# Prompt q and k split by tokens and transposed by DMA in a hybrid streaming step

## The chip, the cores and the metric

The kernel runs on one core of a Trainium2 chip. The metric is the device time of one execution in microseconds (us). Before the change it is 1780.86 us, the median of three runs (1780.17 to 1781.07).

The engines are named as the profile names them: PE is TensorE's matmul, PEld its loading of the stationary operand, DVE is VectorE, ACT is ScalarE, POOL is GpSimd, and SP is SyncE, which only issues transfers here.

## What is computed

One layer of a streaming encoder serves two groups of requests: a prompt of 1024 tokens and 8 samples of 16 tokens, 1152 tokens together. Cut to what the change touches:

```python
h = rms_norm(x, norm_g) * (1 + scale) + shift
proj = h @ w_in                       # q | k | v | gates | SSD inputs ...
q = rms_norm(q.reshape(b, s, 16, 64), q_norm_g)
k = rms_norm(k.reshape(b, s, 16, 64), k_norm_g)
# prompt: each chunk of 64 frames sees its own and the 8 chunks before it
s = einsum('bqhd,bkhd->bhqk', q, k) * 64 ** -0.5 + bias
p = softmax(where(mask, s, -1e30))
o_att = einsum('bhqk,bkhd->bqhd', p, v)
```

The rest of the layer is a gated attention projection, a Mamba-2 scan branch (SSD) with a causal convolution, merge gates, an output projection and the residual. Among the outputs are the last 512 normalised rows of k for the prompt and those of the 128 sample tokens. All of it is float32.

## The kernel before

**Products.** To keep float32 accuracy, a dense product is three fp16 matmuls: high by high, high by low and low by high parts, where the low part is the number less its rounded high part. `dense` (L683, matmuls in L698, L699 and L701) gives channels on the partitions in groups of 384 tokens, `dense_tok` (L737, L751 to L753) tokens on the partitions in blocks of 128. Weights come in 512 KB pieces, `w_split` and `halves` (L610, L619) make the parts, and `level` (L604) squares and sums each piece for a range test at the end.

**Attention by units.** `attention(u)` (L1171) handles two heads, eight units in all. It has four coroutines:

- `dense_gen` projects q, k and v for nine blocks of 128 tokens (eight of the prompt, one of the samples) into `qk` and `v`, then the next unit's gate `z`. The ninth block reuses the first block's place in `qk`, so its eviction is held until `st["turned"]` says that the first half has been turned.
- `prelude` (L1217 on) runs three times, for blocks 0 to 3, 4 to 7 and 8. Pool takes the inverse root of the mean square (`rsqrt_small`, L574) and multiplies the block by it (L1229). For the first two, TensorE transposes q and k (L1249, four 128x128 float32 transposes to a PSUM tile `g`), ScalarE writes the high part with the norm weight as its scale (L1250), once more the k output for the second half (L1252), and VectorE the low part (L1253). The high and low parts of q and k lie in four places `q` of 1024 columns, which are one set: the next unit gets them when this unit's last scores (m = 7) are done. The third run transposes the sample block (L1265) for sample attention and sends the k output (L1276).
- `prompt` (L1302) works in six rounds (`ROUNDS`): scores (L1404) into PSUM, VectorE's negated sum with the bias and its minimum (L1300), ScalarE's exponentials (L1297); then `turn` (L1321) splits the probabilities in two fp16 parts (L1332, L1333) and transposes them by DMA from SP (L1339), and `weigh` multiplies them with v (L1357).
- `sample` does the same for the samples in float32; its probabilities go through one DMA transpose as two 16-bit planes (L1481) and a copy that puts the planes together (L1483), before L1492.

After the eight units come the SSD head, the sixteen SSD pairs and the output stages, which the change does not touch.

**Order of the work.** The coroutines run against a made-up clock: `yield` adds a cost in ns, `pause` waits on that clock, and `walloc` waits for a place of a fixed layout (`L_ATT`, `L_Q`, `L_V` and others, tags such as `T` for v and z, `S` for scores, `Q` for `qk`). That gives a program order. The class `Order` (L137 to L408) then plans the order of each engine's instructions again with a cost model of engines, PSUM slots (three `d`, three `g`, one `s`) and DMA, looking at most 1200 units of work ahead; `cuts` mark where a score or weighing group begins. Each engine then runs its order strictly, waiting on semaphores.

A second kernel, `general_kernel`, follows behind a branch and is entered only if the range test fails; it is not entered here.

Of the kernel before, what the change touches and what calls it, by code (L numbers as in the profile page):

```python
# [16 lines left out]
P = 128  # L17
D = 1024
KT = D // P
NP = 1024  # L20
# [118 lines left out]
class Order:  # L139
# [89 lines left out]
    def build(self):  # L229
# [60 lines left out]
        opener = {}  # L290
        for name, (tag, us) in tiles.items():
# [120 lines left out]
def trunk_kernel(ctx: ExitStack, tc: tile.TileContext, h, again):  # L412
# [71 lines left out]
    L_Q = arena.set_layout(Q0, [("q", 4, 512)])  # L484
# [16 lines left out]
    L_ATT["Q"] = L_ATT["Q"] + arena.set_layout(E0 + 1184 + NP, [("Q", 1, 2048)])["Q"]  # L501
    L_ST = rarena.set_layout(0, [("b", 4, P), ("s", 2, P), ("x", 2, 2 * P)])

    def alloc(lay, tag, cols):
        if lay is L_H or lay is L_W or lay is L_W3 or lay is L_Q or lay is L_V:
            return Buf(arena, arena.alloc(lay, tag, cols // 2), cols, True)
# [538 lines left out]

    pinning[0] = False
# [124 lines left out]
    def attention(u):  # L1171
# [43 lines left out]
        def prelude():  # L1215
            bias = []
            for i, (t0, n) in enumerate(((0, 4), (4, 4), (8, 1))):  # L1217
# [10 lines left out]
                x = qk.ap[:, o0:o0 + 2 * n * P].rearrange("p (h d) -> p h d", d=HD)  # L1228
                nc.gpsimd.tensor_tensor(x, x, v[1].unsqueeze(2).to_broadcast([P, w, HD]), ALU.mult)  # L1229
                yield from pause(2600 + 190 * w + 640 * n)  # L1230
                if i == 0:

                    ops = []
                    for _ in range(4):
                        ops.append((yield from walloc(L_Q, "q", NP)))
                    qh, ql, kh, kl = st["ops"] = ops
                    ko = yield from walloc(lay, "S", 640)
# [4 lines left out]
                if i < 2:  # L1242
                    tok = slice(t0 * P, (t0 + n) * P)
                    for j, (hi, lo) in enumerate(((qh, ql), (kh, kl))):
                        g = par["qk_g"][:, j:j + 1]
                        ps = pg()
                        for s in range(n):
                            o = o0 + (2 * s + j) * P
                            nc.tensor.transpose(ps[:, s * P:(s + 1) * P], qk.ap[:, o:o + P], ident)  # L1249
                        nc.scalar.activation(hi.r[:, tok], ps, AF.Copy, scale=g)  # L1250
                        if i and j:
                            nc.scalar.activation(ko.ap[:, :512], ps, AF.Copy, scale=g)  # L1252
                        nc.vector.scalar_tensor_tensor(lo.r[:, tok], ps, g, hi.ap[:, tok], ALU.mult, ALU.subtract)  # L1253
                        yield 109 * n
                        yield from pause(600)
                    st["turned"] = True
                else:
# [10 lines left out]
                    for e in range(2):  # L1268
                        hs = slice(HD * e, HD * e + HD)
                        nc.scalar.activation(q4[hs, :, e, :], ps[hs, :P].rearrange("p (b s) -> p b s", s=NS), AF.Copy,  # L1270
                                             scale=par["qk_g"][hs, 0:1])
                    nc.scalar.activation(ko.ap[:, 512:], ps[:, P:], AF.Copy, scale=par["qk_g"][:, 1:2])
                    nc.scalar.activation(ks.ap, ps[:, P:], AF.Copy, scale=par["qk_g"][:, 1:2])
# [5 lines left out]
                    nb.free()  # L1279
                    st["bias"] = bias  # L1280
# [21 lines left out]
        def prompt():  # L1302
            yield from ready(lambda: "left" in st and prompts[0] == u)
            yield from until(st["t"])
            qh, ql, kh, kl = st["ops"]
# [41 lines left out]
            def weigh(js, po):  # L1347
# [2605 lines left out]
```

## Time and profile before

| | |
|---|---|
| median of three runs | 1780.86 us |
| the profiled execution | 1782.14 us, its span 1780.1 us |
| busy in the span: PE, DVE, ACT, POOL | 1743.0, 1234.7, 957.6, 351.1 us |
| DMA queue q1 (from SP), share of 16 engines | 51.7% |
| TensorE transposes of q and k (L1249) | 128 instructions, from 79.3 to 571.0 us |
| DMA transposes of probabilities (L1339, L1481) | 128 and 16 instructions, from 112.5 to 634.8 us |

The profile is of one execution. The span runs from the first to the last instruction. A group's row gives its line, engine, operation and shapes, then the busy time of the group and the mean of one instruction, then the engine's idle time just before the group and what ended it. Matmuls overlap, so the time that a matmul takes from the engine is read from the distance of two starts, not from its own length. The digits of the slices are tenths of a fortieth of the span (44.5 us).

### The profile page before, as it was taken

Reading aid. Unit: us, or ns where it says so; the run is one execution under the profiler, and the core shown is the slowest. Engines: PE = TensorE matmul, PEld = TensorE weight load, DVE = VectorE, ACT = ScalarE, POOL = GpSimd, SP = SyncE. Lnnn points to the kernel's source line nnn. Section 1 sums busy time; section 2 is a strip of 40 time slices with the busy share of each in tenths; the row PEclk is TensorE's granted clock in tenths of the full one; section 3 lists DMA queues with packets and bytes.
Section 4 is the critical chain, followed back from the end, with each engine's and each line's share of the span. In section 5 each row is a group of like instructions: output and inputs, shape, how many; then the busy total and the mean of one; then the engine's idle time right before and its main releaser. Section 6 shows DMA issues by size and latency. Waiting matters only on the chain.

```text
span 1780.1 us, 34953 instructions
## 1 busy us (share of the span) xinstructions
PE 1743.0 (98%) x13821; PEld 1095.7 (62%) x13821; DVE 1234.7 (69%) x2327; ACT 957.6 (54%) x1903; POOL 351.1 (20%) x624
## 2 busy tenths in 40 slices
PE   7999999999999999999999999999999999999997
PEld 4556555556655566666666666666666556666664
DVE  6468777885787957786768777777775526876722
ACT  8766556565565666545655666355552615332510
POOL 0233332224314101122212132222122100000000
PEclk9999999999999999999999999999999999999999
DMA  9248978887787984533444545434477734311321
GB/s 381 69 124 222 220 186 204 185 212 199 176 236 166 207 218 129 154 89 116 134 140 137 147 142 165 127 111 129 148 220 292 270 104 154 101 48 57 122 101 56
DMA packets 266565, 284.87 MB, mean 160 GB/s; under 512 B 199628, under 2 KB 200664, under 8 KB 266392
## 3 DMA queue, kind: packets, MB, share of 16 engines
q1 hardware_dynamic: 257432, 253.90, 51.7%
q0 software_dynamic: 8960, 28.65, 4.3%
q8 instruction: 110, 1.80, 0.4%
q14 instruction: 63, 0.52, 0.1%
HBM read 192.70 MB, written 43.66 MB: 133 GB/s over the span
## 4 chain that ended last, share of the span: by engine, by line
PE 81%; ACT 7%; DMA 5%; DVE 3%; POOL 2%; issue 1%; SPq 0%; DVEq 0%; ACTq 0%; POOLq 0%
PE d L698 17%; PE d L699 17%; PE d L701 17%; PE d L751 5%; PE d L753 4%; PE d L752 4%; PE g L1357 2%; PE s L1844 1%; PE g L1816 1%; ACT arena L1743 1%; DMA arena<-arena 1%; PE g L1864 1%; PE s L1404 1%; DMA arena<-in_wall_dram 1%; PE g L1404 1%
## 5 line engine op out<-in xcount | busy, mean ns | idle before, releaser
L698 PE MATMUL d<-arena 128*128 128x384 f16 x2172 | 709.9, 327 | 2.9 <-DVE arena L1714 2.7
L699 PE MATMUL d<-arena 128*128 128x384 f16 x2172 | 708.9, 326 | 0.0
L701 PE MATMUL d<-arena 128*128 128x384 f16 x2172 | 708.8, 326 | 0.0
L701 PEld LDWEIGHTS <-arena 128*128 128x128 f16 x2280 | 223.3, 98 | 148.0 <-issue 0.8
L698 PEld LDWEIGHTS <-arena 128*128 128x128 f16 x2280 | 223.7, 98 | 146.9 <-issue 8.6
L699 PEld LDWEIGHTS <-arena 128*128 128x128 f16 x2280 | 223.4, 98 | 140.6 <-issue 4.1
L608 ACT ACTIVATE arena<-arena 128x1024 bf16<-128x1024 f32 (+3 forms) x169 | 181.6, 1075 | 202.7 <-DMA arena<-in_wall_dram 138.9
L617 DVE SCALAR_TENSOR_TENSOR arena<-arena 128x1024 f16<-128x1024 f32 (+1 forms) x117 | 149.1, 1275 | 81.2 <-ACT arena L616 74.5
L616 ACT ACTIVATE arena<-arena 128x1024 f16<-128x1024 f32 (+1 forms) x117 | 122.4, 1047 | 126.3 <-PE d L699 111.1
L751 PE MATMUL d<-arena 128*128 128x384 f16 (+1 forms) x568 | 186.9, 329 | 0.7 <-ACT arena L1193 0.7
L753 PE MATMUL d<-arena 128*128 128x384 f16 (+1 forms) x568 | 186.1, 328 | 0.0
L752 PE MATMUL d<-arena 128*128 128x384 f16 (+1 forms) x568 | 186.1, 328 | 0.0
L1297 ACT ACTIVATE arena<-arena 128x640 f32<-128x640 f32 (+4 forms) x144 | 100.7, 701 | 66.1 <-DVE arena L1300 65.9
L1555 DVE SCALAR_TENSOR_TENSOR arena<-arena 128x1176 f32<-128x1176 f32 x72 | 107.2, 1488 | 1.9 <-ACT arena L1552 0.5
L1743 ACT ACTIVATE arena<-arena 128x128 f32<-128x128 f32 x288 | 89.7, 389 | 26.1 <-DMA arena<-acs_d 25.9
L1333 DVE SCALAR_TENSOR_TENSOR arena<-arena 128x640 f16<-128x640 f32 (+4 forms) x128 | 87.9, 720 | 0.0
L751 PEld LDWEIGHTS <-arena 128*128 128x128 f16 x576 | 56.2, 98 | 49.7 <-issue 16.4
L1225 POOL TENSOR_SCALAR arena<-arena 128x16 f32<-128x16 f32 (+1 forms) x24 | 11.2, 468 | 366.4 <-DVE arena L1198 331.4
L753 PEld LDWEIGHTS <-arena 128*128 128x128 f16 x576 | 56.4, 98 | 38.4 <-issue 0.2
L1192 ACT ACTIVATE arena<-d 128x256 f32<-128x256 f32 x71 | 26.9, 378 | 95.7 <-PE d L753 95.7
L752 PEld LDWEIGHTS <-arena 128*128 128x128 f16 x576 | 56.4, 98 | 32.7 <-issue 0.6
L1749 DVE TENSOR_TENSOR arena<-arena 128x1152 f32<-128x1152 f32 x32 | 45.9, 1434 | 39.2 <-ACT arena L1747 39.2
(242 smaller groups left out, 2619.5 us busy)
## 6 DMA issues: line engine op xcount, KB each, us to landing
arena<-in_wall_dram SPq DMA_DIRECT2D x85, 512.0 KB
arena<-acs_d SPq DMA_DIRECT2D x32, 576.0 KB
arena<-in_kc_dram SPq DMA_DIRECT2D x64, 256.0 KB
arena<-in_vc_dram SPq DMA_DIRECT2D x64, 256.0 KB
arena<-in_wada_dram SPq DMA_DIRECT2D x24, 512.0 KB
arena<-in_xT_dram SPq DMA_DIRECT2D x16, 576.0 KB
arena<-eacs_d SPq DMA_DIRECT2D x32, 288.0 KB
gate_d<-arena POOLq DMA_DIRECT2D x48, 192.0 KB, 4.2
```

What stands on the lines that cost most here:

```text
L608: keep(nc.scalar.activation(junk[:, :n], x, AF.Square, scale=scale * n ** -0.5, accum_out=sums[:, c:c + 1]))
L616: keep(nc.scalar.activation(hi, x, AF.Copy, scale=scale))
L617: keep(nc.vector.scalar_tensor_tensor(lo, x, scale, hi, ALU.mult, ALU.subtract))
L698: nc.tensor.matmul(ps, hi.r[:, wc], kh.r[:, tok], start=k == 0, stop=False)
L699: nc.tensor.matmul(ps, hi.r[:, wc], kl.r[:, tok], start=False, stop=False)
L701: nc.tensor.matmul(ps, lo.r[:, wc], kh.r[:, tok], start=False, stop=k == nk - 1)
L751: nc.tensor.matmul(ps, kh.r[:, tok], wh, start=k == 0, stop=False)
L752: nc.tensor.matmul(ps, kh.r[:, tok], wl, start=False, stop=False)
L753: nc.tensor.matmul(ps, kl.r[:, tok], wh, start=False, stop=k == KT - 1)
L1297: nc.scalar.activation(p, p, AF.Exp, bias=sm_[:, 4 + e:5 + e], scale=-1.0, accum_out=sm_[:, 6 + e:7 + e])
L1555: nc.vector.scalar_tensor_tensor(yc, r.ap[:, j:j + n], w4[:, i, j:j + 1], yc, ALU.mult, ALU.add)
L1743: nc.scalar.activation(me[e].ap[:, cs], me[e].ap[:, cs], AF.Relu, scale=-1.0, bias=a4[:, c, hds[e]:hds[e] + 1])
```

## The change

- q and k stay with tokens on the partitions until they are split. After the inverse root, Pool multiplies the block by the norm weights as well (a new tile `gains` with the weights repeated over the partitions, q's already times 64 ** -0.5). ScalarE makes the high part and VectorE the low part from `qk` into a new place `y` (two of them, 16 × 128 fp16 columns).
- Two DMA transposes per half (high and low parts, 128 × 1024 each) put them into one place `q` for all four operands, ordered by half of the tokens, part, q or k. TensorE's transposes of the prompt, their copies from PSUM and the k output's copy go. The sample block is still transposed by TensorE.
- The k output goes out with tokens on the partitions, from `qk`, in two stores per unit; the host puts the axes in order.
- The scores' pieces are cut at the border of the halves: 384 + 256, 256 + 384 and 128 + 512 columns for the query blocks 5, 6 and 7, where it was 320 + 320.
- Two more places `T` for v and z. The new places lie where the SSD part has places of its own later.
- `Order.build`: a `g` tile that begins with a marked group now counts the operands of all its matmuls before its first one may be placed.
- `general_kernel` transposes its k output once more, to the same layout; it isn't entered.

```diff
+            members[name] = tag, us
...
+        for name, (tag, us) in members.items():
+            if any(x.name in self.cuts for x in units[us[0]]["ins"]) and tag == "g":
+                for j in us[1:]:
+                    if units[j]["eng"] == "PE":
+                        for k, kind in units[j]["pred"].items():
+                            if k not in us and k < us[0]:
+                                units[us[0]]["pred"].setdefault(k, kind)
...
-    L_Q = arena.set_layout(Q0, [("q", 4, 512)])
+    L_Q = arena.set_layout(Q0, [("q", 1, 2048)])
...
+    L_Y = arena.set_layout(E0 + 1184 + NP + 2048, [("y", 2, 1024)])
+    L_ATT["T"] = L_ATT["T"] + arena.set_layout(E0 + 1184 + NP + 4096, [("T", 2, NT)])["T"]
+    L_G = arena.set_layout(E0 + 1184 + NP + 4096 + 2 * NT, [("g", 1, 256)])
...
+    gains = alloc(L_G, "g", 2 * P)
+    dma(gains.ap, h["gains"])
+    nc.vector.tensor_scalar(gains.ap[:, :P], gains.ap[:, :P], HD ** -0.5, None, ALU.mult)
...
-                x = qk.ap[:, o0:o0 + 2 * n * P].rearrange("p (h d) -> p h d", d=HD)
-                nc.gpsimd.tensor_tensor(x, x, v[1].unsqueeze(2).to_broadcast([P, w, HD]), ALU.mult)
-                yield from pause(2600 + 190 * w + 640 * n)
+                x = qk.ap[:, o0:o0 + 2 * n * P]
+                xh = x.rearrange("p (h d) -> p h d", d=HD)
+                nc.gpsimd.tensor_tensor(xh, xh, v[1].unsqueeze(2).to_broadcast([P, w, HD]), ALU.mult)
+                xt = x.rearrange("p (t c) -> p t c", c=2 * P)
+                nc.gpsimd.tensor_tensor(xt, xt, gains.ap.unsqueeze(1).to_broadcast([P, n, 2 * P]), ALU.mult)
+                yield from pause(2600 + 190 * w + 1100 * n)
...
                 if i < 2:
-                    tok = slice(t0 * P, (t0 + n) * P)
-                    for j, (hi, lo) in enumerate(((qh, ql), (kh, kl))):
-                        g = par["qk_g"][:, j:j + 1]
-                        ps = pg()
-                        for s in range(n):
-                            o = o0 + (2 * s + j) * P
-                            nc.tensor.transpose(ps[:, s * P:(s + 1) * P], qk.ap[:, o:o + P], ident)
-                        nc.scalar.activation(hi.r[:, tok], ps, AF.Copy, scale=g)
-                        if i and j:
-                            nc.scalar.activation(ko.ap[:, :512], ps, AF.Copy, scale=g)
-                        nc.vector.scalar_tensor_tensor(lo.r[:, tok], ps, g, hi.ap[:, tok], ALU.mult, ALU.subtract)
-                        yield 109 * n
-                        yield from pause(600)
+                    y = yield from walloc(L_Y, "y", 16 * P)
+                    c = slice(0, 8 * P), slice(8 * P, 16 * P)
+                    xj = x.rearrange("p (t j d) -> p j t d", j=2, d=P)
+                    yh, yl = (y.r[:, k].rearrange("p (j t d) -> p j t d", j=2, d=P) for k in c)
+                    for j in range(2):
+                        nc.scalar.activation(yh[:, j], xj[:, j], AF.Copy)
+                        nc.vector.tensor_tensor(yl[:, j], xj[:, j], yh[:, j], ALU.subtract)
+                    yield from pause(2500)
+                    for k in c:
+                        o = slice(2 * NP * i + k.start, 2 * NP * i + k.stop)
+                        dma(st["ops"].r[:, o].bitcast(U16).rearrange("p (i k) -> p i k", k=P), y.r[:, k].bitcast(U16), transpose=True)
+                    y.free()
+                    if i:
+                        dma(h["out_k"][u][:, :512].rearrange("p (t d) -> p t d", d=P), xj[:, 1])
+                    yield from pause(4000)
                     st["turned"] = True
...
-                    dma(h["out_k"][u], ko.ap)
-                    stored(ko)
+                    dma(h["out_k"][u][:, 512:], qk.ap[:, P:2 * P])
                     qk.free()
...
+            def part(w, j, at, n):
+                o = at // 512 * 2 * NP + w * NP + j * 512 + at % 512
+                return ops[:, o:o + n]
...
-                (((4, 512, 128, 0, 0), (5, 0, 320, 0, 128), (5, 320, 320, 1, 0)), (0, 1, 2)),
-                (((6, 0, 320, 0, 0), (6, 320, 320, 1, 0)), (3,)),
-                (((7, 0, 320, 0, 0), (7, 320, 320, 1, 0)), (4, 5)),
+                (((4, 512, 128, 0, 0), (5, 0, 384, 0, 128), (5, 384, 256, 1, 0)), (0, 1, 2)),
+                (((6, 0, 256, 0, 0), (6, 256, 384, 1, 0)), (3,)),
+                (((7, 0, 128, 0, 0), (7, 128, 512, 1, 0)), (4, 5)),
```

More of the change, by code (lines that the diff above doesn't have):

```diff
@@ L1398, in prompt @@
                 for m, c, w, k, o in pieces:
[L1399 to L1401 removed]
+                    k0 = max(m - 4, 0) * P + c
+                    for i, (a, b) in enumerate(((0, 0), (0, 1), (1, 0))):
+                        x, y = part(a, 0, m * P, P), part(b, 1, k0, w)
                         for e in range(2):
                             hs = slice(HD * e, HD * e + HD)
[L1404 removed]
+                            mm_ = late(nc.tensor.matmul(banks[k][e][:, o:o + w], x[hs], y[hs], start=i == 0, stop=i == 2))
                             if i == e == 0:
@@ L3008, in prelude @@
                     yield from pause(900)
+                    for k in range(0, 5, 4):
+                        n_ = min(4, 5 - k)
+                        ps = pg(n_ * P)
+                        for s in range(n_):
+                            nc.tensor.transpose(ps[:, s * P:(s + 1) * P], ko.ap[:, (k + s) * P:(k + s + 1) * P], ident)
+                        nc.scalar.activation(ko.ap[:, k * P:(k + n_) * P], ps, AF.Copy)
+                        yield 600
+                    yield from pause(900)
                     dma(h["out_k"][u], ko.ap)
```

30 lines of the change are left out of this document (11 added, 19 removed).

## The prediction

> **What bounds the kernel now.** I read the page first: the engine totals, then the slices.
>
> ```profile
> span 1780.1 us, 34953 instructions
> PE 1743.0 (98%) x13821; PEld 1095.7 (62%) x13821; DVE 1234.7 (69%) x2327; ACT 957.6 (54%) x1903; POOL 351.1 (20%) x624
> PE   7999999999999999999999999999999999999997
> DMA  9248978887787984533444545434477734311321
> ```
>
> TensorE is busy 1743.0 of 1780.1 us, in every slice but the first and the last. So whatever takes matmul time away shortens the kernel, and whatever makes TensorE wait lengthens it. The DMA row shows where a wait could come from: slices 3 to 15 stand at 7 to 9 tenths, and these are the attention units that the change works in. A table of stages says it more finely (stretch; length; busy time and instructions of PE, PEld, DVE, ACT and POOL; granted clock; DMA share; GB/s):
>
> ```profile
> 100.00:150.00 50.00, 50.00 (x481) 29.70 (x480) 37.37 (x112) 29.73 (x77) 15.16 (x22) 1.00 0.64 140
> 150.00:200.00 50.00, 48.97 (x476) 28.54 (x475) 39.73 (x115) 28.58 (x73) 8.17 (x16) 1.00 0.88 223
> 200.00:250.00 50.00, 49.94 (x504) 30.07 (x502) 37.32 (x94) 30.95 (x74) 21.86 (x37) 1.00 0.83 210
> 250.00:300.00 50.00, 49.66 (x518) 31.39 (x516) 37.20 (x86) 28.63 (x66) 21.48 (x37) 1.00 0.80 188
> 300.00:350.00 50.00, 46.77 (x491) 27.63 (x490) 40.13 (x120) 24.40 (x69) 7.44 (x12) 1.00 0.91 204
> 350.00:400.00 50.00, 49.50 (x479) 29.22 (x477) 39.59 (x113) 32.62 (x79) 14.66 (x26) 1.00 0.85 202
> 400.00:450.00 50.00, 49.02 (x500) 30.23 (x501) 31.14 (x79) 28.70 (x69) 22.12 (x37) 1.00 0.77 202
> 450.00:500.00 50.00, 50.00 (x481) 30.51 (x473) 39.61 (x98) 28.48 (x68) 19.16 (x30) 1.00 0.78 173
> 500.00:550.00 50.00, 48.99 (x536) 27.61 (x534) 42.47 (x119) 27.38 (x77) 10.16 (x19) 1.00 0.92 235
> 550.00:600.00 50.00, 47.53 (x438) 27.86 (x437) 41.92 (x107) 34.48 (x80) 14.12 (x29) 1.00 0.72 168
> 600.00:650.00 50.00, 49.69 (x510) 31.23 (x508) 38.01 (x75) 27.82 (x52) 4.21 (x14) 1.00 0.92 219
> sum 550.00, PE 540.06 PEld 324.00 DVE 424.49 ACT 321.76 POOL 158.54; mean PE 49.10 PEld 29.45 DVE 38.59 ACT 29.25 POOL 14.41
> ```
>
> TensorE idles 9.9 us in these 550; the DMA shares average 0.82, 451 us of all 16 engines. The stage has little TensorE time to win back but what is taken out of it, and 99 us of DMA room. The change moves work from the full engine to the second fullest resource.
>
> **The change, part by part.** *Transposes taken from TensorE.* The groups by line (busy, mean ns of one, then idle before them) and the row of one run of eight with what follows it:
>
> ```profile
> L1249 PE MATMUL g<-arena 128*128 128x128 f32 x128 | 18.3, 275 | 2.3 <-POOL arena L1229 2.3
> ...
> 209.57 1.04 PE L1249 MATMUL g<-arena 128*128 128x128 f32 x8
> 210.44 0.27 PE L1504 MATMUL g<-arena 128*128 128x128 f32 x1
> ```
>
> Eight start at 209.57 and the next matmul at 210.44: 0.87 us, 109 ns each. (The mean of 275 has the drain in it, which the next matmul overlaps.) 128 × 109 ns = 13.9 us go. TensorE also stood idle 2.3 us ahead of them for Pool's normalisation; only the two transposes of the sample tokens (L1265) still wait on that line, so I take these 2.3 us as gone too. Together −16.2 us.
>
> *DMA transposes added.* Per unit two halves of the tokens times a high and a low part: 4 × 8 = 32, each 128 rows of 1024 two-byte numbers, 256 KB or 1024 packets of 256 bytes. The DMA view of 112 to 120 us, where five older transposes (L1339) run and nothing else does, gives the price of a packet, and the source view of L1339 that of an issue on SP's queue (min/median/max):
>
> ```profile
> DMA packets 2076, 0.52 MB, mean 65 GB/s; under 512 B 2074, under 2 KB 2074, under 8 KB 2074
> ...
> q1 hardware_dynamic: 2074, 0.50, 32.8%
> ...
> arena<-arena SPq DMA_TRANSPOSE x5
> ...
> L1339 SPq DMA_TRANSPOSE arena<-arena x128: 1167/1344/4386, 112.5 to 630.3; - x128
> ```
>
> 0.328 × 16 × 8 us = 42 engine-us for 2074 packets is 20.2 ns each. 32 × 1024 × 20.2 ns / 16 = 41 us of all engines. SP issues for 32 × 1.34 = 43 us more; what queues behind such an issue, or behind its wait for the split, are the other units' transposes, the cached keys and values, and the weights. The DMA load of the stage becomes 451 + 41 = 492 us in 550 − 14 = 536, a share of 0.92. The page "DMA: Bandwidth & Descriptors" of the Trainium skill, section "Latency and other measured facts", has 261 GB/s for a transpose with a non-contiguous middle dimension; 8.4 MB at that rate would be 32 us and a share of 0.90, an estimate that the 20.2 ns per packet of this trace (12.7 GB/s an engine, 203 in all) does not bear out.
>
> What a full DMA does to TensorE is in the trace once. From the chain (start, length), VectorE's row and TensorE's:
>
> ```profile
> 296.23 8.56 DMA arena<-arena
> ...
> 304.88 0.88 DVE L1483 COPY arena<-arena 128x1280 uint16<-128x1280 uint16 x1 [2.52 <-DMA arena<-arena]
> ...
> 306.02 0.85 PE L1492 MATMUL g<-arena 128*32 128x128 f32 x22 [3.23 <-DVE arena L1483]
> ```
>
> One transpose took 8.56 us to land, and TensorE stood 3.23 us behind the copy that needed it. It is not in every full stretch: the three at 0.91 and 0.92 have 3.23, 1.01 and 0.31 us of idle, 1.5 on average; the other eight 0, 1.03, 0.06, 0.34, 0.50, 0.98, 0 and 2.47, 0.7 on average. If the added transposes lift those eight to the load of the three, that costs 8 × 0.85 = +6.8 us. Ends: 0 (the eight are as late as before) and one wait of 3.23 us in each of the eight units, +25.8. I take 6.8, since it is read from stretches that run at the very share I expect.
>
> *Splitting, norm weights, stores.* Rows:
>
> ```profile
> L1250 ACT ACTIVATE arena<-g,arena 128x512 f16<-128x512 f32 x32 | 20.9, 677 | 2.8 <-PE g L1249 2.6
> L613 ACT ACTIVATE arena<-arena 128x512 f16<-128x512 f32 x16 | 10.1, 629 | 0.0
> L1253 DVE SCALAR_TENSOR_TENSOR arena<-g,arena 128x512 f16<-128x512 f32 x32 | 23.5, 744 | 6.2 <-ACT arena L1250 3.9 <-ACT arena L1252 2.1
> L614 DVE TENSOR_TENSOR arena<-arena 128x512 f16<-128x512 f32 x16 | 11.2, 703 | 0.9 <-ACT arena L613 0.2
> L1229 POOL TENSOR_TENSOR arena<-arena 128x1024 f32<-128x1024 f32 x16 | 31.4, 1960 | 0.1
> L1229 POOL TENSOR_TENSOR arena<-arena 128x256 f32<-128x256 f32 x8 | 5.1, 641 | 0.2
> ```
>
> 32 ScalarE copies of 677 ns become 32 of 629 (the split of v, L613, has that shape), 32 VectorE subtractions of 744 ns become 32 of 703 (L614), and ScalarE's copies for the k output go. ScalarE and VectorE are busy 322 and 424 of the 550 us, so I count nothing. Pool multiplies each normalised block once more: 16 × 1.96 + 8 × 0.64 = 36.5 us, on an engine that is busy 158 of the 550: nothing, but 2 us later in each prelude. The k output in two stores per unit is as many bytes and 8 more issues: nothing. The `gains` load of 128 KB comes before the attention stage and nothing waits for it before the first prelude: nothing.
>
> *A longer prelude.* By the pauses in the code the next unit's q and k are ready later: 6.5 us after the q place is free where it was 2.1, and with the second half and the sample block some 11 us in sum. TensorE's rows at such a change of units (last scores, first transposes, first scores of the next):
>
> ```profile
> 342.76 0.57 PE L1404 MATMUL g<-arena 64*128 64x320 f16 x6
> ...
> 345.32 0.60 PE L1249 MATMUL g<-arena 128*128 128x128 f32 x4
> ...
> 371.23 0.67 PE L1404 MATMUL s<-arena 64*128 64x128 f16 x12
> ```
>
> 28 us lie between the units' scores, and TensorE is busy 49.5 of the 50 us from 350: the dense products of the next units fill it. With two more places for v and z they may run further ahead, and the split no longer writes into q's place, so a token block's eviction waits for less than before. Cost 0, with that cover; without it the bounds are −1.5 us (the idle of 350 to 450, if it closes) and +11 us in each of seven units. I take 0, by the 49.5.
>
> *Scores cut at 128, 256, 384 and 512 instead of 320*, and the planner's rule that a score bank's first matmul is placed when all its operands are ready: the same columns in the same number of matmuls, 0. The second part can only move a wait; bounds ±2.5 us (the idle of 550 to 600, closed or doubled), taken as 0, the middle.
>
> **Sum.** −13.9 − 2.3 + 6.8 = −9.4 us. The profiled execution took 1782.14 us, 2.0 beyond its span of 1780.1; its span would become 1770.7 and it 1772.7. It lies 1.3 over the median of 1780.86, so for the median I say 1771.5.
>
> **Rivals.** *A, the DMA keeps up.* The added transposes are hidden as the old ones are, of which the waits name little (total, times, longest):
>
> ```profile
> PE g L1357 <- DMA arena<-arena: 0.8, 2, 0.5
> ```
>
> Then −16.2 us: 1764.7. For it, besides, the 99 us of room; against it the three full stretches.
>
> *B, late transposes are the new bound: slower.* Every unit's scores wait for q and k that come through a queue at 0.92, as late as the 8.56 us above. One wait of 3.23 us where there was none, doubled because each unit has two halves to wait for: 8 × 2 × 3.23 = 51.7 is the far end; one per unit gives 25.8 − 16.2 = +9.6, 1790.5. It decides from 16.2 / 8 = 2.0 us per unit. For it: the share, and the single q place, which lets no transpose start before the last scores of the unit before. Against it: the stretch of 500 to 550 ran at 0.92 with 1.01 us of idle.
>
> *C, Pool holds VectorE.* The trace has VectorE stuck beside a Pool multiplication:
>
> ```profile
> 470.49 1.90 POOL L1229 TENSOR_TENSOR arena<-arena 128x1024 f32<-128x1024 f32 x1
> ...
> 470.68 2.52 DVE L1332 TENSOR_SCALAR arena<-arena 128x640 f16<-128x640 f32 x2
> ...
> L1332 DVE TENSOR_SCALAR arena<-arena x128: 272/510/2191, 111.7 to 626.5; 128x640 f16<-128x640 f32 x64, 128x128 f16<-128x128 f32 x16, 128x256 f16<-128x256 f32 x16, 128x384 f16<-128x384 f32 x16
> ```
>
> Two instructions with a median of 510 ns took 2.52 us, 1.5 too long. If each of the 16 long new multiplications held one and TensorE waited it out, 16 × 1.5 = 24 us come back, +7.8 in all: 1788.7. It decides from 1.0 us per multiplication. Against it: 450 to 500, where this stands, has TensorE at 50.00 of 50. The page "SBUF — State Buffer" of the Trainium skill, section "Who interferes with whom", says that VectorE in a two-port mode or with two SBUF inputs and GpSimd exclude each other for the whole instruction; the 2.52 us agree, and the new subtraction from SBUF is of that kind while the old one read PSUM.
>
> *D, nothing comes of it.* The planner deals the order of all engines anew, and late waits happen to take what the transposes leave: within 3.6 us of 1780.9.
>
> **How the numbers follow.** Forecast 0.45, with a range of its own of 1766 to 1777; A 0.17; B 0.22; C 0.06; D 0.10. 0.2% is about what a measurement of this kernel can tell from no change, 3.6 us. Faster: forecast and A, 0.62. Same: D, 0.10. Slower: B and C, 0.28. The range goes from 1763, just under A, to 1790, where half of B lies beyond: some 0.08 is left out below and 0.11 above.
>
> **What would show it.** In the changed kernel L1249's line has no TensorE matmul; 32 more DMA transposes stand at SP, with a median issue near 1.34 us; the DMA share of the attention stage is near 0.92; Pool is busy 36 us more; TensorE's idle in the stage is near 15 us (9.9 + 6.8, less what it waited for Pool). The forecast is wrong upward if TensorE's waits name DMA transposes or scores by several us per unit, downward if its idle falls below the present 9.9.

## The result and the profile after

The changed kernel is slower: 1790.6 us, median of 13 runs (1785.3 to 1794.35), beside 1780.65 us for the kernel before in the same runs (1775.3 to 1788.68). The ratio is 1.0053, 95% interval 1.0038 to 1.0068. The prediction said 1771.5 and a range up to 1790, so it has the sign wrong and ends 0.6 us short of the result. The profiled execution took 1790.7 us, its span 1788.9. Ratios leave out three slow executions (one each of a_high, a_norule and the kernel before), which move the medians below by at most 0.15 us.

The page of the changed kernel: span, engine totals, DMA slices.

```profile
span 1788.9 us, 34710 instructions
PE 1734.1 (97%) x13693; PEld 1080.7 (60%) x13693; DVE 1251.5 (70%) x2328; ACT 949.0 (53%) x1887; POOL 399.1 (22%) x648
...
DMA  9248899899899895543554365434567734311331
```

The whole loss shows in TensorE's total. TensorE is busy 8.9 us less than before (1743.0 to 1734.1), yet idle 1788.9 − 1734.1 = 54.8 us where it was 1780.1 − 1743.0 = 37.1: +17.7. −8.9 + 17.7 = +8.8, the difference of the spans. Where the idle time lies is in the table of stages (columns as in the prediction's; the sum of 100 to 650 is worked out below it):

```profile
100.00:150.00 50.00, 47.38 (x369) 27.02 (x367) 32.36 (x83) 27.60 (x73) 21.58 (x32) 0.97 0.43 95
150.00:200.00 50.00, 46.78 (x471) 28.14 (x470) 40.69 (x95) 22.59 (x60) 19.14 (x28) 1.00 0.96 211
200.00:250.00 50.00, 47.78 (x469) 27.11 (x467) 42.77 (x109) 30.92 (x73) 17.40 (x27) 1.00 0.95 216
250.00:300.00 50.00, 49.19 (x541) 29.25 (x540) 42.17 (x102) 27.84 (x66) 28.31 (x39) 1.00 0.94 216
300.00:350.00 50.00, 47.43 (x408) 27.19 (x406) 33.08 (x96) 27.06 (x73) 14.76 (x18) 1.00 0.93 217
350.00:400.00 50.00, 47.31 (x527) 28.81 (x526) 41.79 (x100) 24.40 (x61) 22.36 (x37) 1.00 1.01 214
400.00:450.00 50.00, 49.24 (x478) 27.88 (x476) 41.87 (x101) 30.98 (x71) 20.89 (x30) 1.00 0.91 206
450.00:500.00 50.00, 45.09 (x458) 25.58 (x457) 34.48 (x97) 28.64 (x76) 19.78 (x26) 1.00 0.85 194
500.00:550.00 50.00, 49.26 (x454) 27.82 (x453) 36.96 (x99) 22.29 (x64) 19.02 (x28) 1.00 1.02 234
550.00:600.00 50.00, 47.15 (x445) 26.86 (x440) 38.41 (x95) 31.04 (x71) 21.09 (x34) 1.00 1.00 219
600.00:650.00 50.00, 48.76 (x504) 29.30 (x503) 46.83 (x114) 27.81 (x56) 2.28 (x6) 1.00 0.79 180
650.00:700.00 50.00, 45.02 (x395) 29.33 (x390) 31.39 (x58) 30.89 (x62) 4.89 (x13) 0.93 0.77 179
```

From 100 to 650 TensorE idles 24.6 us (9.9 before), and 5.0 in the stretch from 650 (0.3 before), which still weighs values. No stretch is without idle, where before two were full. What it waits for is in TensorE's waits from 100 to 700 us (total, times, longest):

```profile
PE s L1423 <- DVE arena L1314: 11.5, 11, 2.2
PE s L1478 <- DVE arena L1314: 3.5, 2, 2.6
PE d L709 <- ACT arena L1551: 3.3, 4, 1.2
PE g L1423 <- DVE arena L1529: 3.0, 3, 1.5
```

No DMA transpose is named. The scores (L1423, the L1404 of before; L1478 are those of the samples, L1459 before) wait for the PSUM tile `s`, of which there is one, until VectorE's negated sum (L1314, before L1300) has read the scores in it. VectorE is late. The groups that tell why (busy, mean ns of one, idle before), after:

```profile
L1352 DVE SCALAR_TENSOR_TENSOR arena<-arena 128x640 f16<-128x640 f32 (+4 forms) x128 | 98.8, 801 | 0.0
L1351 DVE TENSOR_SCALAR arena<-arena 128x640 f16<-128x640 f32 (+4 forms) x128 | 66.5, 555 | 9.6 <-DMA arena<-arena 8.8 <-PE g L1376 0.3
L1246 POOL TENSOR_TENSOR arena<-arena 128x1024 f32<-128x1024 f32 (+1 forms) x24 | 48.9, 2036 | 1.6
L1244 POOL TENSOR_TENSOR arena<-arena 128x1024 f32<-128x1024 f32 (+1 forms) x24 | 40.9, 1703 | 0.2
```

and the same of before, which has no second multiplication:

```profile
L1333 DVE SCALAR_TENSOR_TENSOR arena<-arena 128x640 f16<-128x640 f32 (+4 forms) x128 | 87.9, 720 | 0.0
L1332 DVE TENSOR_SCALAR arena<-arena 128x640 f16<-128x640 f32 (+4 forms) x128 | 59.2, 500 | 1.1
L1229 POOL TENSOR_TENSOR arena<-arena 128x1024 f32<-128x1024 f32 (+1 forms) x24 | 36.5, 1521 | 0.2
```

The same 256 instructions of VectorE, the split of the probabilities in `turn`, take 165.3 us instead of 147.1, +18.2. Pool's normalisation takes 1703 ns instead of 1521, and its new multiplication by the norm weights (L1246) 2036 ns on the same shapes. VectorE and Pool slow each other. One such place from the timeline (start, length):

```profile
217.20 2.49 POOL L1246 TENSOR_TENSOR arena<-arena 128x1024 f32<-128x1024 f32 x1
...
217.59 2.77 DVE L1352 SCALAR_TENSOR_TENSOR arena<-arena 128x640 f16<-128x640 f32 x1
...
220.36 0.40 DVE L1314 CUSTOM_DVE_ANT_0 arena<-s,arena 128x256 f32<-128x256 f32 x1
...
221.24 0.34 PE L1423 MATMUL s<-arena 64*128 64x128 f16 x6 [2.22 <-DVE arena L1314]
```

VectorE's split starts 0.39 us after Pool's multiplication and ends at 220.36, 0.67 us after Pool's end; the negated sums queue behind it, and TensorE, whose next instruction needs the tile that they read, stands 2.22 us. This is rival C's mechanism. Four theories remained to be told apart: **P**, Pool's multiplication holds VectorE (the expectations below call it C, as the prediction did); **L**, the DMA engines are too full; **W**, the longer way of q and k through one place `q`; **R**, the planner's rule for `g` tiles moves the scores for the worse.

### The profile page after: what moved, and what is told of

The parts are those of the page before. It is cut to its first block, busy times and chain, and to the rows that moved or that the text cites. A ratio compares the mean times of both kernels' runs of the same rounds, so it can differ in the third digit from the quotient of the medians.

```text
span 1788.9 us, 34710 instructions
## 1 busy us (share of the span) xinstructions
PE 1734.1 (97%) x13693; PEld 1080.7 (60%) x13693; DVE 1251.5 (70%) x2328; ACT 949.0 (53%) x1887; POOL 399.1 (22%) x648
## 4 chain that ended last, share of the span: by engine, by line
PE 59%; DVE 3%; DMA 2%; ACT 1%; issue 1%; SPq 0%; DVEq 0%
PE d L709 16%; PE d L710 16%; PE d L712 16%; PE g L1835 2%; PE s L1863 2%; PE g L1883 1%; PE g L710 1%; PE g L712 1%; PE g L709 1%; DMA arena<-in_wall_dram 1%; PE g L1870 1%; PE g L1908 1%; DVE arena L1574 1%; PE g L1699 0%; DMA arena<-arena 0%
## 5 line engine op out<-in xcount | busy, mean ns | idle before, releaser
L628 DVE SCALAR_TENSOR_TENSOR arena<-arena 128x1024 f16<-128x1024 f32 (+1 forms) x117 | 145.4, 1243 | 49.7 <-ACT arena L627 47.9
L1762 ACT ACTIVATE arena<-arena 128x128 f32<-128x128 f32 x288 | 90.1, 389 | 21.1 <-DMA arena<-acs_d 20.9
L1352 DVE SCALAR_TENSOR_TENSOR arena<-arena 128x640 f16<-128x640 f32 (+4 forms) x128 | 98.8, 801 | 0.0
L1351 DVE TENSOR_SCALAR arena<-arena 128x640 f16<-128x640 f32 (+4 forms) x128 | 66.5, 555 | 9.6 <-DMA arena<-arena 8.8
L1314 DVE CUSTOM_DVE_ANT_0 arena<-s,arena 128x128 f32<-128x128 f32 (+4 forms) x128 | 57.3, 476 | 19.7 <-DMA arena<-in_bias_dram 7.9
```

The costliest lines, as they stand in the source:

```text
L628: keep(nc.vector.scalar_tensor_tensor(lo, x, scale, hi, ALU.mult, ALU.subtract))
L1352: nc.vector.scalar_tensor_tensor(y[:, n * P:], p, r[:, e:e + 1], y[:, :n * P], ALU.mult, ALU.subtract)
```

## The experiments

Names with a_ are the changed kernel with an edit, names with b_ the kernel before with an edit; a_dve2_norule and its like carry two. Ratios are to the kernel before, run beside each; its medians there lie between 1779.24 and 1780.73 us, so a difference between two edited kernels carries up to some 1.5 us of that.

**The transposes alone.** In b_idle_tr the kernel before issues the 32 DMA transposes as well, into a place that nothing reads; b_idle_ld puts 32 plain loads, meant to take the same engine time, in their stead.

```diff
+y = yield from walloc(L_Y, "y", 16 * P)
+for k in range(2):                               # b_idle_tr
+    dma(y.r[:, k * 1024:(k + 1) * 1024].bitcast(U16).rearrange("p (i k) -> p i k", k=P),
+        qk.ap[:, o0 + 512 * k:o0 + 512 * k + 512].bitcast(U16), transpose=True)
+    dma(y.ap.bitcast(F32)[:, :864], h["xT"][k][:, :864])    # b_idle_ld, in its stead
+y.free()
```

> The kernel before, with 32 more DMA transposes of 128x1024 two-byte numbers: two per half and unit, from SP, out of the block's own place into a place that nothing reads. TensorE's transposes stay, so nobody waits for the new ones. Theory L (the DMA engines are over-full, and what they carry is late whatever it is): the change lost 10 us net and took 14 us of TensorE work away, so the load alone costs about 24: 1805 us (1793 to 1815). Theory W (the scores wait for q and k because these come later, through a longer chain; the load by itself does little): at most 1785 us.

> The kernel before, with 32 more plain loads of 128x864 float32 (442 KB, some 41 us of all engines, as the 32 transposes have) in place of the idle transposes, into the same unread places. Theory L with the engines' time as what counts: as slow as with the idle transposes, 1805 us (1793 to 1815). If SP's time to issue a transpose (1.3 us against 0.34 us for a load) is what counts: about 1785 us. Theory W: at most 1785 us.

Measured: b_idle_tr 1791.58 us, ratio 1.0061 [1.0038, 1.0084], +10.9 us; b_idle_ld 1779.13, 0.9993 [0.9982, 1.0003], nothing. The DMA queue from 100 to 650 us (packets, MB, share of 16 engines), of the kernel before, of b_idle_tr and of b_idle_ld:

```profile
q1 hardware_dynamic: 179694, 107.14, 81.2%
```

```profile
q1 hardware_dynamic: 208870, 112.94, 89.9%
```

```profile
q1 hardware_dynamic: 182857, 114.81, 86.0%
```

The loads brought 4.8 points of the 8.7, not as much as was meant, and not at the same times. They wait for no result, so the planner put 16 of the 32 before 100 us and the last at 370.3; the transposes were issued from 79.2 to 577.3. From 100 to 370 us the loads raised the queue's share nearly as much (80.7% before, 88.9% with the loads, 89.7% with the transposes), and the loads cost nothing. From 370 to 650 the shares are 81.7, 83.3 and 90.1%, and there b_idle_ld is no test. So L in its plain form, busy engines make everything late, is not borne out where it was tested.

The transposes cost 0.34 us each although nothing reads what they write. They differ from the loads in one more way: they read `qk`, so SP, which issues in order, stood 7.7 us in five waits before them for Pool's normalisation (the loads stood 13.3 us for their place, and cost nothing). The profiled span is 9.2 us longer: TensorE idles 4.7 us more and is busy 4.5 us longer, of which some 3.5 us are a lower granted clock (last section).

Is it SP's time to issue? b_idle_sp adds 128 loads of 2 KB on SP:

```diff
+for k in range(8):
+    dma(y.ap.bitcast(F32)[:, 128 * k:128 * k + 4], h["xT"][k][:, :4])
```

> The kernel before, with 128 tiny loads (2 KB each) from SP in place of the 32 idle transposes: some 45 us more of SP's issue time, as the transposes take, and hardly any of the DMA engines' bytes. Theory S (an idle transpose cost 0.34 us each because SP, which issues in order, is held): as slow as with the idle transposes, 1789 to 1794 us. Theory X (the transposing itself holds up the DMA queues: 256-byte packets behind which everything else lands late): 1778 to 1784 us.

1782.64 us, 1.0022 [1.0008, 1.0036]: +3 us for 128 issues. That is a small part of the 10.9 us. These loads too were placed early, from 37.2 to 377.7 us, so for the rest of the stage it is not shown.

**Half of the transposes, and fewer loads beside them.** a_high transposes the high parts alone, and the scores read them in the low parts' place too; a_novc drops the 64 loads of cached v, and the samples read the cached k instead.

```diff
-for k in c:
+for k in c[:1]:                                  # a_high
...
-x, y = part(a, 0, m * P, P), part(b, 1, k0, w)
+x, y = part(0, 0, m * P, P), part(0, 1, k0, w)
...
+vcs = kcs                                        # a_novc, the loads of vc taken out
```

> The changed kernel, of whose 32 transposes the 16 of the low parts are left out; the scores read the high parts in their place, so q and k count with their high parts alone and the scores' third product is wrong. Chain, pauses, places and Pool's work stay. Theory L: half of the 24 us comes back, 1778.5 us (1774 to 1783). Theory W: no less than 1787 us.

> The changed kernel without the 64 loads of the cached v (256 KB each, about 50 us of all engines); the samples' product with v reads the cached k instead, so the samples' attention is not the reference's. The path of q and k stays as it is. Theory L: the stage's DMA load falls a little under that of the kernel before, all of the 24 us comes back: 1767 us (1763 to 1773). Theory W: no less than 1786 us.

a_high 1773.39 us, 0.9963 [0.9951, 0.9974]: 17.2 under the changed kernel. a_novc 1782.67, 1.0016 [1.0006, 1.0026]: 7.9 under it. Both are reliefs of the queue, and both lie under the floors that W set (1787 and 1786 us). For L, a_high is 0.6 us beyond its range and a_novc 10 us short of its gain; but a_novc's profiled execution lost 10.2 us to a lower granted clock, twice the changed kernel's 5.1 (last section), so its 7.9 can hide a larger relief. TensorE's largest wait in both still is `s` behind L1314. In a_high, from 100 to 700 us:

```profile
PE s L1423 <- DVE arena L1314: 5.6, 8, 2.0
PE s L1478 <- DVE arena L1314: 4.2, 2, 2.6
```

**One or two places for q and k.** a_q2 gives the transposed operands two places, in the room of the two new places `T`.

```diff
-L_ATT["T"] = L_ATT["T"] + arena.set_layout(E0 + 1184 + NP + 4096, [("T", 2, NT)])["T"]
+L_Q["q"] = L_Q["q"] + arena.set_layout(E0 + 1184 + NP + 4096, [("q", 1, 2048)])["q"]
```

> The changed kernel with a second place for the q and k operands, where the two added places for v and z were, which go. The next unit's transposes need not wait for this unit's last scores. Theory W (the single place and the longer prelude make the scores late): 1786 us or less. Theory T (transposes are late wherever they stand, and every round's probabilities with them): 1788 to 1794 us.

1797.99 us, 1.0101 [1.008, 1.0122]: slower still. W would have had it faster. But the run also takes the places `T` away, and its profiled execution lost some 15 us to a lower granted clock (5.1 in the changed kernel), so it shows only that a second place bought with the places `T` does not help; it does not price the single place by itself.

**Pool's multiplication and the planner's rule, taken out.** a_nogain leaves out the multiplication, so q and k lack the norm weights; a_norule leaves out the rule.

```diff
-xt = x.rearrange("p (t c) -> p t c", c=2 * P)                      # a_nogain
-nc.gpsimd.tensor_tensor(xt, xt, gains.ap.unsqueeze(1).to_broadcast([P, n, 2 * P]), ALU.mult)
...
-for name, (tag, us) in members.items():                            # a_norule
-    if any(x.name in self.cuts for x in units[us[0]]["ins"]) and tag == "g":
-        ...
```

> The changed kernel without Pool's multiplication by the norm weights; q and k of the prompt and the samples lack them. Theory C (Pool's 36 us hold VectorE by the port they share, and TensorE waits): at least 4 us of the 10 come back, 1786.5 us or less. Without C: 1788 to 1793 us.

> The changed kernel without the planner's new rule for the first matmul of a marked g tile. If the rule, which holds scores back until all operands of a tile are planned to be there, is what stretches the scores of a unit (from some 41 us to some 60): 1786 us or less. If not: 1788 to 1795 us.

a_nogain 1772.86 us, 0.9962 [0.9949, 0.9975]: 17.7 under the changed kernel. a_norule 1779.7, 0.9998 [0.9985, 1.001]: 10.9 under it. Each of the two steps that I had set to nothing is worth more than the whole of the forecast's −9.4. In the groups of a_nogain, VectorE's split is 152.5 us, near the 147.1 of before:

```profile
L1350 DVE SCALAR_TENSOR_TENSOR arena<-arena 128x640 f16<-128x640 f32 (+4 forms) x128 | 92.4, 751 | 0.2
L1349 DVE TENSOR_SCALAR arena<-arena 128x640 f16<-128x640 f32 (+4 forms) x128 | 60.1, 502 | 15.1 <-DMA arena<-arena 14.7
```

**Is it only another plan?** Any edit makes the planner deal the order anew. Three runs change nothing but a constant of the plan, and a fourth puts the rule into the kernel before.

```diff
-yield from pause(1300)                           # a_jit1, in the prelude
+yield from pause(1200)
-SAFE_DMA = 2500.0                                # a_jit2
+SAFE_DMA = 2600.0
-SAFE_SLOT = 500.0                                # a_jit3
+SAFE_SLOT = 550.0
...
+for name, (tag, us) in members.items():          # b_rule: the rule, in the kernel before
+    ...
```

> The changed kernel with one pause of the prelude at 1200 instead of 1300 on the made-up clock: no work is added or removed, but the planner deals the order anew. If the losses seen so far are costs of the named parts: within 4 us of the changed kernel, 1787 to 1795 us. If they are mostly the luck of one planned order: 1773 to 1785 us.

> The changed kernel with the planner's margin behind a transfer at 2600 ns instead of 2500; again no work is added or removed. Costs of parts: 1787 to 1795 us. Luck of one order: 1773 to 1785 us.

> The changed kernel with the planner's margin behind a PSUM place at 550 ns instead of 500; again no work is added or removed. Costs of parts: 1787 to 1795 us. Luck of one order: 1773 to 1785 us.

> The kernel before with the planner's new rule for marked g tiles and nothing else of the change. If the rule costs by itself (leaving it out of the changed kernel gave 11 us): 1785 to 1793 us. If it costs only where the operands come by DMA, or if that 11 us was the luck of an order: 1777 to 1784 us.

a_jit1 1788.31 (1.005 [1.003, 1.007]), a_jit2 1788.61 (1.0052 [1.0035, 1.0069]), a_jit3 1791.94 (1.0066 [1.0049, 1.0083]): a new plan alone moved the changed kernel by some 2 us three times. Differences of 10 and more I take for the parts themselves, though an edit that takes work out may deal the order anew by more than a constant does. b_rule 1780.53 (1.0006 [0.9995, 1.0018]): in the kernel before the rule costs nothing, so its 10.9 us come only together with the rest of the change.

**Is Pool's work late, or does it hold VectorE?** In a_gain_idle Pool does the multiplication, in pieces of two token blocks, into a place that nothing reads: nobody can wait for it. b_idle_pool adds such idle multiplications to the kernel before.

```diff
-nc.gpsimd.tensor_tensor(xt, xt, gains..., ALU.mult)
+nc.gpsimd.tensor_tensor(spare[...], xt[:, z0:z1], gains..., ALU.mult)          # a_gain_idle
...
+nc.gpsimd.tensor_tensor(spare[:, :z1 - z0], xt[:, z0:z1], xt[:, z0:z1], ALU.mult)   # b_idle_pool
```

> The changed kernel with Pool's multiplication by the norm weights going into a place that nothing reads, in pieces of 512 columns: Pool works as long as in the changed kernel, but q and k don't wait for it (and lack the weights). Leaving the multiplication out gave 17.7 us. Theory C (Pool holds VectorE by the shared port): little of that comes back, 1785 to 1792 us. Theory D2 (the 2 us that each block waits for it are what costs): most comes back, 1771 to 1777 us.

> The kernel before with as many idle Pool multiplications of the same size beside the path. Theory C: slower by several us, 1784 to 1797 us. Theory D2: 1778 to 1783 us. If C holds only where the units' scores already stand back to back, as in the changed kernel, this one stays at 1778 to 1784 us too, and the idle multiplication in the changed kernel tells.

a_gain_idle 1787.72 us, 1.0047 [1.0033, 1.006]; b_idle_pool 1785.44, 1.0029 [1.0015, 1.0043]. The idle multiplication keeps 14.9 of the 17.7 us that leaving it out had brought, so most of the time goes by what Pool does to its neighbour, not by q and k coming later. (In its 40 pieces it keeps Pool busy 56.8 us, where the real one took 48.9, so 14.9 may be on the high side.) In the kernel before, with 45.0 us of Pool, it costs 6.2 us. The groups of b_idle_pool:

```profile
L1338 DVE SCALAR_TENSOR_TENSOR arena<-arena 128x640 f16<-128x640 f32 (+4 forms) x128 | 92.4, 756 | 0.0
L1337 DVE TENSOR_SCALAR arena<-arena 128x640 f16<-128x640 f32 (+4 forms) x128 | 65.4, 549 | 1.8 <-DMA arena<-arena 0.7
L1234 POOL TENSOR_TENSOR arena<-arena 128x512 f32<-128x512 f32 (+1 forms) x40 | 45.0, 1126 | 2.7
```

The split is 157.8 us here, +10.7, though no data passes between the two.

**The multiplication on other engines.** a_dve does it on VectorE; a_dve_norule does so without the rule; a_dve2_norule has Pool's first multiplication on VectorE too; a_ev_norule, also without the rule, multiplies by the weights when VectorE evicts the projection from PSUM. Nothing is left out in these four.

```diff
-nc.gpsimd.tensor_tensor(xt, xt, gains..., ALU.mult)
+nc.vector.tensor_tensor(xt, xt, gains..., ALU.mult)                # a_dve, a_dve_norule, a_dve2_norule
...
-nc.gpsimd.tensor_tensor(xh, xh, v[1]..., ALU.mult)
+nc.vector.tensor_tensor(xh, xh, v[1]..., ALU.mult)                 # a_dve2_norule
...
-nc.scalar.activation(c, ps[:, :2 * P], AF.Copy, scale=1.0 / SW)
+nc.vector.scalar_tensor_tensor(c, ps[:, :2 * P], 1.0 / SW, gains.ap, ALU.mult, ALU.mult)   # a_ev_norule
```

> The changed kernel without the planner's rule, and with the same multiplication of whole blocks by VectorE in Pool's place, some 24 us of VectorE's time that keeps its place in the prelude. If it was Pool's port: 1763 to 1774 us. If the wait of the block was what cost: 1776 to 1782 us, as without the rule alone.

> The changed kernel without the planner's rule, and with the norm weights multiplied in by VectorE as q and k leave PSUM (in place of ScalarE's copy; ScalarE's squares read PSUM), so Pool's second multiplication goes and nothing of the result is left out. If the two costs are separate (17.7 and 10.9 us) and VectorE's 72 longer evictions cost little: 1762 to 1770 us, faster than both kernels. If both relieve the same chain: about 1772 us. If VectorE becomes the bound: 1780 us or more.

> The changed kernel, planner's rule included, with the multiplication by the norm weights on VectorE in Pool's place and nothing else altered. Theory C, with the port as the cost: most of the 17.7 us that leaving it out gave comes back, 1770 to 1778 us. If the rule costs its 11 us whatever Pool does: 1774 to 1780 us. If the two only cost together: 1766 to 1770 us, as without the rule.

> As the best version so far (1767.3 us: without the rule, norm weights on VectorE), with Pool's first multiplication, by the inverse root, on VectorE as well. If Pool's long operations still hold VectorE: 1758 to 1765 us. If TensorE has nothing left to wait for in this stage (0.2 us of idle from 100 to 580 us): 1765 to 1769 us. If VectorE's 24 us more make it late: 1770 us or more.

a_dve_norule is the fastest kernel of this study: 1767.3 us, 0.9931 [0.9914, 0.9947], some 12 us under the kernel before and 23 under the changed one. a_ev_norule 1774.34 (0.9972 [0.9962, 0.9982]), a_dve2_norule 1773.65 (0.9964 [0.995, 0.9977]), a_dve 1780.52 (1.0001 [0.9984, 1.0018]). Moving the multiplication to VectorE is worth 10.1 us with the rule (1790.6 to 1780.5) and 12.4 without (1779.7 to 1767.3); the rule costs 10.9 with Pool and 13.2 with VectorE. Here the two add up. The second move to VectorE gives 6.4 back. In a_dve_norule, the groups, then the windows, then the DMA queue from 100 to 650:

```profile
L1345 DVE SCALAR_TENSOR_TENSOR arena<-arena 128x640 f16<-128x640 f32 (+4 forms) x128 | 89.0, 726 | 0.1
L1239 DVE TENSOR_TENSOR arena<-arena 128x1024 f32<-128x1024 f32 (+1 forms) x24 | 22.9, 956 | 18.0 <-POOL arena L1237 18.0
```

```profile
100.00:580.00 480.00, 479.79 (x4683) 275.78 (x4681) 373.70 (x992) 271.20 (x683) 164.34 (x265) 1.00 0.96 214
```

```profile
q1 hardware_dynamic: 214789, 113.80, 92.0%
```

TensorE is busy 479.79 of 480 us while the DMA engines stand at 0.96. All 32 transposes are there and are waited for, and the DMA is fuller than in the changed kernel (88.4%). This ends L as a general bound, for this kernel at least: a full DMA does not make TensorE wait by itself. The multiplication takes VectorE 956 ns, less than half of Pool's 2036.

The same window shows what the other kernels lose. TensorE's idle in it is 480 less the first busy time; VectorE's split is the sum of its two groups. Both are of one profiled execution each, while the times are medians; a_dve and a_norule were profiled at 1776.57 and 1776.72 us:

| kernel | us | TensorE idle, 100 to 580 | VectorE's split |
|---|---|---|---|
| before | 1780.65 | 8.7 | 147.1 |
| changed | 1790.6 | 22.5 | 165.3 |
| a_gain_idle | 1787.72 | 17.5 | 161.2 |
| a_dve | 1780.52 | 11.8 | 149.0 |
| a_norule | 1779.7 | 5.7 | 155.6 |
| a_high | 1773.39 | 11.7 | 157.0 |
| a_nogain | 1772.86 | 9.1 | 152.5 |
| a_dve_norule | 1767.3 | 0.2 | 147.4 |

In the changed kernel and its variants the time goes with the idle time, within some 7 us. The four edits that remove one load each bring 17.7, 17.2, 10.9 and 7.9 us, 53.7 in all, where only 22.5 us of idle are there: they are not four separate costs. As I read it they shorten one chain: VectorE's split, its DMA transposes, and the negated sum that frees the tile `s`, which waits behind the split on VectorE. No run shows that by itself. Nor is the split's time alone the cause: a_norule, with all of Pool's work, has 155.6 us of split and 5.7 of idle, a_nogain 152.5 and 9.1.

## Why the prediction was wrong

*TensorE's transposes, −13.9.* Right as to the work: L1249 has no TensorE matmul any more. Right also that the gain can be had: a_dve_norule's span is 1768.0, 12.1 under that of before. But busy time fell by 8.9 only. Of the other 5.0, some 1.7 are a lower granted clock (5.1 us lost here, 3.4 before; last section). The row of the sample scores grew from 17.1 us (L1459 in before) to 20.0 (L1478), but a row's sum holds the drains that the next matmul overlaps: by the distance of starts it is 114 ns a matmul before and 123 now, about 1 us over 128. The rest I can't place.

```profile
L1478 PE MATMUL s<-arena 128*32 128x512 f32 x128 | 20.0, 605 | 4.5 <-DVE arena L1314 3.5 <-DMA arena<-in_kc_dram 1.0
```

```profile
L1459 PE MATMUL s<-arena 128*32 128x512 f32 x128 | 17.1, 605 | 0.0
```

*Waits for Pool, −2.3.* Gone from TensorE's list, as said.

*DMA, +6.8.* Mis-sized, and argued from the wrong quantity. The share of the stage rose from 0.82 to 0.89, near the 0.92 expected, and issues took 1.43 us at the median where I had 1.34:

```profile
L1266 SPq DMA_TRANSPOSE arena<-arena x32: 1237/1426/3957, 82.7 to 588.0; - x32
```

But the share by itself says little: a_dve_norule idles 0.2 us at 0.96. What the transposes cost depends on the rest of the kernel: 10.9 us when idle in the kernel before, 17.2 for half of them in the changed one, while a_dve_norule has all of them and TensorE hardly waits.

*"Pool multiplies each normalised block once more … : nothing".* **The first step that failed.** I asked whether Pool had time, and it had. I did not price what Pool's time does to VectorE, though the row of 470.68 stood in the prediction. Pool's second multiplication took 48.9 us, not 36.5, and it costs the changed kernel 10.1 us (against VectorE doing it) to 17.7 (against leaving it out).

*The planner's rule: bounds ±2.5, "taken as 0, the middle".* **The second.** It costs 10.9 us in the changed kernel (13.2 with the multiplication on VectorE); the bound came from one stretch's idle, though the rule acts on the order in all eight units; b_rule shows that alone, in the kernel before, it is in fact nothing. Weighing tells how far the order is pushed back. The source views of the changed kernel and of a_dve_norule (min/median/max ns, first to last start):

```profile
L1376 PE MATMUL g<-arena x1440: 219/219/243, 141.5 to 669.2; 128*64 128x128 f16 x180
```

```profile
L1369 PE MATMUL g<-arena x1440: 219/219/244, 137.4 to 647.8; 128*64 128x128 f16 x180
```

The last weighing starts at 669.2 us where it was 647.8; a_norule has 656.7, before 639.9. By its text the rule lets a score group wait for the operands of all its matmuls; with q and k in halves it would wait for the second half. That is argued from the code and not tried.

*The longer prelude, 0.* Not refuted: no wait of TensorE names the new transposes. a_q2 doesn't price the prelude by itself. The new cut of the scores was not tried alone.

*Rivals.* B's price, 1790.5, is the measured time, but for another reason: TensorE's waits name VectorE, not late transposes of q and k. C had the mechanism and 1788.7 for it, and I gave it 0.06. The argument against it, that TensorE was busy 50.00 of 50 us beside one such collision, showed only that dense products covered that one; where the scores come next, as at 221.24, nothing covered it. The rule of the page "SBUF — State Buffer" of the Trainium skill, section "Who interferes with whom", that VectorE in a two-port mode, or with two SBUF inputs beside a GpSimd instruction that reads SBUF, and GpSimd shut each other out for a whole instruction, agrees with the pair at 217.20 and 217.59; b_idle_pool, where no data passes between the two, fits it as well. A and D fell: the DMA keeps up in a_dve_norule, but not by itself, and three new plans moved the time 2 us, not 10.

## What to carry to other kernels

Before work is put on a Pool that looks free, ask which VectorE instructions run beside it and who waits for them: here a long Pool multiplication was paid for by VectorE, and through a single PSUM tile by TensorE. Price every edit at the planner by the whole stage that it reorders, and try it apart from the rest: here two side edits hid a gain of 12 us behind a loss of 10. Reliefs of one stage need not add up: the four taken singly promise 53.7 us where 22.5 are idle. Moving the multiplication and leaving the rule out did add up, and only a run of both could tell.

## What was not expected of the hardware

**A stall can cost more than its length.** After a wait of 2.62 us TensorE ran at half pace. The timeline (start, length):

```profile
131.23 1.06 PE L1478 MATMUL s<-arena 128*32 128x512 f32 x8 [2.62 <-DVE arena L1314]
...
132.94 0.53 PE L763 MATMUL d<-arena 128*128 128x384 f16 x1
133.26 0.53 PE L764 MATMUL d<-arena 128*128 128x384 f16 x1
...
135.71 0.33 PE L763 MATMUL d<-arena 128*128 128x384 f16 x1
135.87 0.33 PE L764 MATMUL d<-arena 128*128 128x384 f16 x1
```

and two windows of 3.5 us, granted clock third from the end:

```profile
131.00:134.50 3.50, 3.27 (x22) 1.32 (x23) 3.50 (x13) 1.49 (x5) 0.00 (x0) 0.67 0.76 122
134.50:138.00 3.50, 3.50 (x20) 1.98 (x19) 3.27 (x8) 1.78 (x4) 0.00 (x0) 0.84 0.99 319
```

Starts lie 0.32 us apart and then 0.16. Taken as half speed, 0.67 and 0.84 stand for 2 × (0.33 + 0.16) × 3.5 = 3.4 us, so another 1.7 us were lost. The page "TensorE: Matmul & The Clock Gate" of the Trainium skill, section "Part 1: The HAM clock gate (the "warmup" mystery)", puts the half clock after an idle window of about 3.4 us; here a wait of 2.62 us went before it. The length of one wait does not decide it. In a_jit1 a wait of 2.23 us at the same scores (to 221.70) is followed by 0.51 from 222 to 225 us; in the changed kernel the wait of 2.22 us (to 221.24) is followed by 1.00; and the 3.23 us of the kernel before (to 306.02) by 1.00 too. Two waits of 1.43 and 1.34 us in the changed kernel, to 677.19 and 679.16, came before twice as long a dip.

This is a part of the differences above. In windows of 5 us from 0 to 1765, length × (1 − granted clock) adds up to 3.4 us in the kernel before, 5.1 in the changed one, 6.9 in b_idle_tr, 10.2 in a_novc, some 15 in a_q2 and 1.7 in a_nogain: close to multiples of 1.7. These are of the profiled executions.

**An idle transpose is not free.** 32 of them cost the kernel before 10.9 us, though nothing reads what they write. Plain loads cost nothing with nearly the same rise in share up to 370 us, and 128 small issues on SP 3 us; but both were placed earlier than the transposes, and neither waits for Pool. So it is open whether transposing costs more than loading, or when it is issued and what SP waits for.
